# The FFN of a decoder block by 2x2 blocks with seven block products, its inner layer kept in DRAM

## The chip, the core and the metric

The kernel runs on one core of a Trainium2 chip. The metric is the device time of one execution in microseconds. The engines named below are TensorE (PE: matrix products into PSUM; PEld is its weight load), VectorE (DVE), ScalarE (ACT), GpSimd (POOL) and SyncE (SP, which here issues the DMA transfers).

## The reference

One decoder layer on x of 1024 tokens by 1024 channels, in float32: three token mixers, gated and merged, an output projection, and then the part that the change touches, a convolutional gated MLP of 2816 inner channels:

```python
    x = x + rms_norm(mixed @ w_out[l], post_mix_norm[l])
    h = rms_norm(x, pre_ffn_norm[l])
    u = causal_dwconv(h @ ffn_w_up[l], ffn_conv_w[l], ffn_conv_b[l])   # [1024, 5632], 3 taps along the tokens
    gate, val = jnp.split(u, 2, axis=-1)
    f = (jax.nn.gelu(gate, approximate=True) * val) @ ffn_w_down[l]    # [1024, 2816] @ [2816, 1024]
    x = x + rms_norm(f, post_ffn_norm[l])
```

## The kernel before

Everything is kept transposed: channels on the 128 partitions, the 1024 tokens along the free dimension, in two halves of 512. [...] `load_w` loads one unit of weights by an SP DMA, takes hi on ACT (L269) and lo on POOL (L270), or on DVE where it is given its tiles. `fm_unit` runs the matmuls of one unit of 128 output channels over `nk` input tiles (L205 is the helper that records each).

`tail_stage` holds the merge of the branches, the output projection with its norms (by halves of the sequence; the rows of x1 go to DRAM as `x1_d`), and the FFN. The FFN's input is `h2[h, k]`, a (hi, lo) pair for each half h and input tile k of 8. The inner layer has 22 tiles of 128 channels. For tile f, `up` takes two units, gate and value: 8 k x 3 matmuls x 2 halves each, 96 in all; then the convolution of three taps (`conv`: ACT L303 for the first tap, DVE L307 and L309 for the two others, `halo` being the columns that the second half needs of the first), the gelu on ACT (L1338), the product on DVE (L1345), and the split into `mhi` and `mlo` (L1346, L1347), which stay in SBUF. `down(ci, ms)` follows each chunk of `DOWN`: eight units of output channels, `nf` x 3 matmuls x 2 halves each, added to `acc` in SBUF by DVE (L1358; the first chunk is copied by ACT, L1356). The products of chunk 16 to 17 are run last but one, after the last tile's `up`; the last chunk is run by pieces of the sequence (`LAST`: 512, 256, 256 tokens), each followed by the last norm, the residual from `x1_d` and the output.

The first four tiles (`N_FIRST`) are run by halves, because the second half of the sequence is still being normalised. Within each engine the order is set by a scheduler that goes by the order of the program text, dependencies and a timeline of its own; pools of tiles (`bufs`) decide how far an engine can run ahead. All the FFN's loads go through the one queue of SP, in order.

Of the kernel before, what the change touches and what calls it, by code (L numbers as in the profile page):

```python
# [27 lines left out]
# columns of the per-channel parameter table  # L28
# [12 lines left out]
def consts():  # L41
# [18 lines left out]
    # rows 64..127 of the keys' operand: position, ones, blocks, ones for the two maxima  # L60
# [7 lines left out]
    # the queries' side of position and ones, [q, tile, head, 3], each exact in bfloat16  # L68
# [5 lines left out]
    # bias of the compressed scores, [g, tile, q, head, 64]; slot 0 is empty  # L74
# [5 lines left out]
    # blocks that are always or never taken: factor and addend, [tile, q, 2, 16]  # L80
# [12 lines left out]
def layout(a):  # L93
    """The arrays as the program takes them: transposed, cut and repeated only."""
    def units(w, cols, width=128):
        # [k*128+p, cols] -> [unit, p, k*width+c]
        w = w[:, cols]
        k = w.shape[0] // 128
        u = w.shape[1] // width
        return np.ascontiguousarray(  # L100
            w.reshape(k, 128, u, width).transpose(2, 1, 0, 3).reshape(u, 128, k * width))

    def per_channel(v):
        # [..., n*128] -> [128, n * ...]
        v = v.reshape(-1, v.shape[-1] // 128, 128) if v.ndim > 1 else v.reshape(1, -1, 128)
        return v.transpose(2, 1, 0).reshape(128, -1)
# [21 lines left out]
    # parameters by channel, in the order of the units  # L128
# [13 lines left out]
    # down: [chunk, unit, p, k*128+c], chunks of DCH tiles of the hidden layer  # L142
# [16 lines left out]
DOWN = [(0, 4), (4, 4), (8, 4), (12, 4), (16, 2), (18, 4)]  # L159
# [3 lines left out]
# The merge gates' projection units: up to which one they go with the sparse attention, the heads of the  # L163
# stick-breaking attention and the groups of the state space mixer.
# [3 lines left out]
# steps of projections traced with each step of the mixers, and the order of the latter's units  # L168
# [22 lines left out]
# the output: after which tile of a piece the one before is finished, and the tiles of one transfer  # L191
T_AT = 3
T_DMA = ((0, 4), (4, 8)), ((0, 2), (2, 4), (4, 6), (6, 8))
# [3 lines left out]
def trunk(ctx: ExitStack, tc: tile.TileContext, A: dict, outT: bass.AP, dbg=None):  # L197
# [36 lines left out]
    def rsqrt_mean(r, v, ps, n):  # L234
        """r = (ps / n + eps) ** -0.5, by exp and log and one step of Newton's; v is scratch."""
# [37 lines left out]
    def fm_unit(pool, w, rhs, nk, halves=(0, 1)):  # L273
        """ps[feature, t] of one unit of 128 features, by halves of the sequence; rhs(k, half) -> (hi, lo)."""
# [11 lines left out]
    def half_unit(pool, w, rhs, nk, h, out):  # L286
        """The same of one half, in steps of one k."""
# [12 lines left out]
    def conv(o, h, ps, taps, bias, halo):  # L300
        """o[:, t] = bias + sum of taps[d] * ps[:, t - d], for half h of the sequence; o is its part of the output"""
# [46 lines left out]
    def tm_part(ci, p, eng):  # L348
        """A quarter of the rows of a chunk of the token-major weights"""
# [37 lines left out]
    def first_half(h, tiles):  # L387
        """Input scaled by channel, split, and its squares' sum"""
# [22 lines left out]
    def norm(h, ss):  # L411
        """By token: the scale of the queries, and of the input on every partition"""
# [35 lines left out]
    def unit_steps(u, evict):  # L448
        """A projection unit by halves; a step is one half with what takes it from PSUM."""
# [6 lines left out]
    def fine_steps(u, evict):  # L456
        """The same, a step being one k of a half."""
# [6 lines left out]
    class Fill:  # L464
        """Projection steps, traced between those of the mixers."""
# [28 lines left out]
    eac = keep.tile([128, 8, 16], F32, name="eac")       # exp of the log-decay from the chunk's start  # L494
    eend = keep.tile([128, 8, 16], F32, name="eend")     # the same of the whole chunk, on every partition
# [49 lines left out]
def nsa_stage(nc, tc, es, env, start):  # L545
# [4 lines left out]
    V_hi = kp.tile([128, 8, 2, 2, 65], R32, name="V_hi")  # [key, tile, sel/win, group, value | 1]  # L550
# [51 lines left out]
    for s in range(2):  # L602
        # two positions at a time: [parity of the position | channel] on the partitions
# [15 lines left out]
        # one row for each block of each group, and one between the groups that nothing uses  # L619
# [27 lines left out]
    # the keys of one group at a time; the second's wait in DRAM  # L647
# [63 lines left out]
    def compressed(g, i):  # L711
# [61 lines left out]
        # the queries' operands of the two other branches  # L773
# [16 lines left out]
    def maxima(g, i):  # L790
        """The rows' maxima, into the operands."""
# [39 lines left out]
    def attend():  # L831
        """Scores by key, weights, values: one block of keys a step, None where there is none."""
# [80 lines left out]
    for n in range(-2, 17):  # L913
# [38 lines left out]
def sb_stage(nc, tc, es, env):  # L952
# [42 lines left out]
    def chain(h, c, ps_z, ps_out, q_hi, q_lo, k_hi, k_lo, v_hi, v_lo):  # L995
        """One head's queries of half c, from the last block of keys to the first."""
# [11 lines left out]
        def strict(x, kb):  # L1008
            # x >= 0, perhaps infinite; zero where the key isn't before the query
# [5 lines left out]
        def score(kb):  # L1015
# [6 lines left out]
            # softplus  # L1022
# [10 lines left out]
        def carry(kb):  # L1033
# [10 lines left out]
            # the softplus of this key and all between it and the query, to be taken from the scores  # L1044
# [50 lines left out]
def ssd_stage(nc, tc, es, env):  # L1095
# [8 lines left out]
    def scan(q, fill, x0, x1, B, C, z0, z1):  # L1104
# [6 lines left out]
        def front(c):  # L1111
# [8 lines left out]
            # token-major x and B, C.B by group  # L1120
# [54 lines left out]
        # gate, norm over the group's 256 channels  # L1175
# [24 lines left out]
def tail_stage(nc, tc, es, env):  # L1200
# [10 lines left out]
    def lo_t(dt=R32):  # L1211
        return mp.tile([128, 512], dt, name="lo", bufs=17)
# [11 lines left out]
    def load_y(k):  # L1224
        # the first ones take the place of what the mixers have done with
# [39 lines left out]
    up_ = es.enter_context(tc.tile_pool(name="up", side="right", reuse_waits="tile", bufs=U_BUFS))  # L1265
    op = ExitStack()
    ow = op.enter_context(tc.tile_pool(name="ow", reuse_waits="tile", bufs=2))
    for h in range(2):
        o = ow.tile([128, 8, 512], F32, name="o")

        def sumsq(sums, src, eng=V):
            """sums[0] += src^2; None for the first"""
# [16 lines left out]
        for j in range(8):  # L1289
            ps, = fm_unit(psd, load_w(A["wo"][j], 1024), lambda k, _: mix[h, k], 8, halves=(h,))  # L1290
            act(o[:, j, :], ps, AF.Copy)
# [3 lines left out]
        for j in range(8):  # L1295
            x = ow.tile([128, 512], F32, name="ox", bufs=8)
            nc.sync.dma_start(x, A["xT"][j * 128:(j + 1) * 128, hs(h)])
            V.scalar_tensor_tensor(o[:, j, :], o[:, j, :], pvc(PV_PM, j), r, op0=OP.mult, op1=OP.mult)
# [23 lines left out]
    def h2_rhs(k, h):  # L1322
        return h2[h, k]

    def up(f, st, halves=(0, 1)):
# [13 lines left out]
        if halves[-1] == 0:  # L1339
            return  # L1340
# [9 lines left out]
    def down(ci, ms, also=None):  # L1350
        nf = DOWN[ci][1]
        for j in range(8):
# [6 lines left out]
            if also:  # L1359
                also(j)  # L1360
# [97 lines left out]
```

## Time and profile before

| | |
|---|---|
| time, median of 3 | 2348.51 us (2346.61 to 2348.75) |
| the profiled execution | span 2347.0 us from the first to the last instruction; no other time was taken of it |
| PE busy | 2261.6 us, 96% |
| DVE, ACT, POOL busy | 1311.3, 1055.4, 912.3 us |
| mean granted TensorE clock | 0.988 |
| DMA, mean over the span | 74 GB/s |
| out-projection and norms | about 1461 to 1640 us |
| FFN | from about 1580 us; its last chunk from about 2275 us |

The profile is of one execution. A row of its groups gives the line, the engine, the operation, output and input tiles, shapes and count, then busy time and the mean of one in ns, then the engine's idle time just before these and what ended it. A window's row gives busy time and number of instructions for each engine. Matmuls are pipelined: a record is longer than the time between two of them. Engines work at the same time, so that busy shares do not add up.

### The profile page before, as it was taken

What the parts mean: (1) busy time and instruction counts of PE and PEld (TensorE: products, weight loads), DVE (VectorE), ACT (ScalarE), POOL (GpSimd) and SP (SyncE); (2) the same over time, 40 slices, a digit from 0 to 9 for tenths busy, and PEclk for the clock granted to TensorE, in tenths of its full rate; (3) what the DMA queues carried; (4) which work ended last, traced back from release to release, by engine and by line L of the source; (5) the groups of instructions that cost most, each with busy time, mean ns of one, the idle gap of its engine ahead of it and who ended that gap; (6) DMA issues with size and microseconds to landing.
All of it is one profiled execution on the core that took longest, in us unless ns stands there. A gap on an engine that the chain in (4) does not pass through costs nothing.

```text
span 2347.0 us, 29315 instructions
## 1 busy us (share of the span) xinstructions
PE 2261.6 (96%) x11020; PEld 1828.0 (78%) x11020; DVE 1311.3 (56%) x2351; ACT 1055.4 (45%) x1842; POOL 912.3 (39%) x671
## 2 busy tenths in 40 slices
PE   8999999999999999999998999998999999999997
PEld 7997666667887788778786888876788888888886
DVE  8324875781476676565757443378714343443556
ACT  7144665666466766444443322345433131322334
POOL 4122565565233324553535264455422221222213
PEclk9999999999999999999999999998999999999998
DMA  5233112101111112021212462343221111112132
GB/s 191 81 88 96 48 40 69 57 8 59 37 54 46 46 45 72 32 77 41 77 53 83 159 202 97 117 152 111 78 63 41 59 41 50 54 32 67 46 117 72
DMA packets 90126, 173.49 MB, mean 74 GB/s; under 512 B 25280, under 2 KB 39296, under 8 KB 89984
## 3 DMA queue, kind: packets, MB, share of 16 engines
q1 hardware_dynamic: 89696, 171.39, 22.4%
q8 instruction: 87, 1.43, 0.2%
q14 instruction: 55, 0.45, 0.1%
q10 hardware_dynamic: 288, 0.22, 0.0%
HBM read 138.55 MB, written 33.03 MB: 73 GB/s over the span
## 4 chain that ended last, share of the span: by engine, by line
PE 82%; DVE 11%; ACT 3%; issue 2%; POOL 2%; DMA 1%; SPq 0%; DVEq 0%; ACTq 0%; POOLq 0%
PE dense L205 66%; PE ps_s L205 5%; PE ps_o L205 4%; PE ps_t L205 4%; PE ps_b L205 2%; DVE mx L813 2%; POOL wlo L270 1%; DVE row L307 1%; DVE o L1306 1%; ACT whi L269 0%; DVE acc L1410 0%; POOL R L1116 0%; DVE xe L1138 0%; POOL osq L1278 0%; DVE cp L733 0%
## 5 line engine op out<-in xcount | busy, mean ns | idle before, releaser
L270 POOL TENSOR_TENSOR wlo<-wraw,whi 128x1024 fp32r<-128x1024 f32 (+2 forms) x194 | 405.5, 2092 | 837.1 <-ACT whi L269 799.7
L205 PE MATMUL dense<-h_hi,whi 128*128 128x512 f32 x992 | 401.6, 405 | 3.5 <-DVE row L307 3.4
L205 PE MATMUL dense<-h_lo,whi 128*128 128x512 f32 x992 | 393.4, 397 | 0.0
L205 PE MATMUL dense<-h_hi,wlo 128*128 128x512 f32 x992 | 392.0, 395 | 0.0
L269 ACT ACTIVATE whi<-wraw 128x1024 fp32r<-128x1024 f32 (+2 forms) x194 | 179.2, 925 | 386.0 <-PE dense L205 350.2
L205 PE MATMUL dense<-hi,whi 128*128 128x512 f32 x832 | 326.6, 393 | 11.2 <-ACT whi L269 11.2
L205 PE MATMUL dense<-hi,wlo 128*128 128x512 f32 x832 | 327.0, 394 | 4.4 <-POOL wlo L270 4.3
L205 PE MATMUL dense<-lo,whi 128*128 128x512 f32 x832 | 326.0, 392 | 1.5 <-POOL lo L1313 1.5
L205 PEld LDWEIGHTS dense<-h_hi,whi 128*128 128x128 f32 x992 | 188.3, 190 | 44.4 <-ACT sa L1026 3.6
L205 PEld LDWEIGHTS dense<-h_hi,wlo 128*128 128x128 f32 x992 | 187.6, 189 | 40.0 <-issue 1.1
L205 PEld LDWEIGHTS dense<-h_lo,whi 128*128 128x128 f32 x992 | 188.3, 190 | 36.0 <-issue 1.8
L307 DVE SCALAR_TENSOR_TENSOR u<-dense,pv,u 128x511 f32<-128x511 f32 (+1 forms) x176 | 130.8, 743 | 133.3 <-ACT u L303 132.0
L853 POOL TENSOR_TENSOR wT_lo<-wT,wT_hi 128x512 fp32r<-128x512 f32 x132 | 169.2, 1292 | 86.7 <-ACT wT_hi L852 80.2
L205 PEld LDWEIGHTS dense<-hi,whi 128*128 128x128 f32 x832 | 157.5, 189 | 46.2 <-ACT whi L269 13.4
L205 PEld LDWEIGHTS dense<-hi,wlo 128*128 128x128 f32 x832 | 157.4, 189 | 40.6 <-POOL wlo L270 7.2
L205 PEld LDWEIGHTS dense<-lo,whi 128*128 128x128 f32 x832 | 157.4, 189 | 35.3 <-POOL lo L1313 2.4
L205 PE MATMUL dense<-mhi,whi 128*128 128x512 f32 x288 | 112.2, 392 | 0.3
L205 PE MATMUL dense<-mlo,whi 128*128 128x512 f32 x288 | 112.3, 390 | 0.0
L1043 POOL TENSOR_TENSOR s_lo<-sa,s_hi 128x512 fp32r<-128x512 f32 (+2 forms) x48 | 53.8, 1125 | 148.9 <-ACT s_hi L1042 137.6
L842 ACT ACTIVATE wT<-ps_s 128x512 f32<-128x512 f32 x132 | 78.4, 594 | 68.3 <-PE ps_s L205 63.6
L205 PE MATMUL dense<-mhi,wlo 128*128 128x512 f32 x288 | 105.6, 389 | 0.0
L813 DVE TENSOR_REDUCE mx<-ps_t 128x1 f32<-128x384 f32 (+3 forms) x192 | 93.9, 514 | 18.1 <-PE ps_t L205 15.9
(377 smaller groups left out, 4560.8 us busy)
## 6 DMA issues: line engine op xcount, KB each, us to landing
wraw<-in_wfm SPq DMA_DIRECT2D x62, 512.0 KB, 3.4
wraw<-in_wup SPq DMA_DIRECT2D x52, 512.0 KB, 3.3
g_d<-gate_e SPq DMA_DIRECT2D x48, 256.0 KB, 2.1
ge<-g_d SPq DMA_DIRECT2D x24, 512.0 KB, 3.9
wraw<-in_wo SPq DMA_DIRECT2D x16, 512.0 KB, 3.4
wraw<-in_wdn SPq DMA_DIRECT2D x32, 256.0 KB, 2.6
yraw<-y_d SPq DMA_DIRECT2D x12, 512.0 KB, 4.2
x<-in_xT SPq DMA_DIRECT2D x16, 256.0 KB, 5.5
```

The lines of the kernel that those rows point to most:

```text
L205: i = f(*a, **k)
L269: act(hi, raw, AF.Copy)
L270: (V if tiles else P).tensor_tensor(lo, raw, fl(hi), op=OP.subtract)
L307: V.scalar_tensor_tensor(o[:, d:], ps[:, :512 - d], taps[d], o[:, d:], op0=OP.mult, op1=OP.add)
L813: V.tensor_reduce(mx[:, h, a, n:n + 1], pm[:, :w], axis=AX, op=OP.max)
L842: act(w.rearrange("p h q -> p (h q)"), pz, AF.Exp)
L853: P.tensor_tensor(lo, wf, fl(hi), op=OP.subtract)
L1043: (P if SB_SLO else V).tensor_tensor(s_lo[:, c0:], a[:, c0:], fl(s_hi[:, c0:]), op=OP.subtract)
L1306: i = V.scalar_tensor_tensor(o[:, j, :], o[:, j, :], pvc(PV_FFN, j), r, op0=OP.mult, op1=OP.mult)
```

## The change

A product of matrices cut into 2x2 blocks needs eight block products; after combining blocks by additions beforehand and adding up the results, seven do. The change uses this twice, with fifteen additions of blocks in its form.

In the up projection the 2x2 blocks of the weights are (gate, value) by (input tiles 0 to 3, 4 to 7), and those of the input are (input tiles 0 to 3, 4 to 7) by (first, second half of the sequence). `up_pair` runs 7 products x 4 tiles x 3 = 84 matmuls for a tile of the inner layer. It does so for 18 of the 22 tiles; the first four are run by halves as before. The combinations of the input are made once (`combos`, on DVE). Those of the weights are made for each tile by `weights7`, the four additions and the lo parts on POOL, the hi parts on ACT. The results are put together in three PSUM banks x, y, z: the bank x goes on collecting products, and ACT copies its state (`snap`) at three points.

All tiles' `up` now comes first. The inner layer goes to DRAM (`m_d`) in float32, half a tile at a time, and is read back chunk by chunk. `DOWN` is cut into chunks of 2, 4, 4, 4, 4 and 4 tiles. For the first five, `m_rhs` combines (POOL) and splits (ACT hi, DVE lo) the inner layer's blocks, and `down_pair` computes two units of output channels at once by seven products: 42 matmuls instead of 48 in a chunk of four, 21 instead of 24 in that of two. The results are added to `acc` by DVE (from PSUM) and by POOL (the copies). The last chunk is run by pieces as before, with its inner layer and weights loaded, and split by ACT and DVE, behind the fifth chunk. x1 is read by two transfers of 2 MB in place of 16 of 256 KB, placed in the SP queue ahead of the last four units' weights; the output leaves by one transfer per unit and piece. The ring of lo tiles has 16 buffers instead of 17, that of the convolution's tiles 4 instead of 6.

The diff, cut to its core (its other lines only remove comments or rename the pieces of the last chunk):

```diff
-DOWN = [(0, 4), (4, 4), (8, 4), (12, 4), (16, 2), (18, 4)]
+DOWN = [(0, 2), (2, 4), (6, 4), (10, 4), (14, 4), (18, 4)]
-U_BUFS = 6
+U_BUFS = 4
...
+    def weights7(src0, src1, n):
+        raws = []
+        for m, src in enumerate((src0, src1)):
+            raw = (wx if turn[0] % 3 == 2 else E.wp).tile([128, 1024], F32, name="wraw", bufs=1 + (turn[0] % 3 < 2))[:, :2 * n]
+            turn[0] += 1
+            nc.sync.dma_start(raw, src)
+            raws.append(raw)
+        a11, a12, a21, a22 = [r[:, s] for r in raws for s in (slice(0, n), slice(n, 2 * n))]
+        whi, wlo = [E.wp.tile([128, 1024], R32, name=f"w{x}", bufs=2)[:, :2 * n] for x in ("hi", "lo")]
+        ahi, alo = [wx.tile([128, 512], R32, name=f"a{x}", bufs=1)[:, :n] for x in ("hi", "lo")]
+        act(whi, raws[0], AF.Copy)
+        P.tensor_tensor(wlo, raws[0], fl(whi), op=OP.subtract)
+        f31, f24 = [wx.tile([128, 1024], F32, name=f"uf{x}", bufs=1)[:, :2 * n] for x in range(2)]
+        (h31, l31), (h24, l24) = [[wx.tile([128, 1024], R32, name=f"u{x}")[:, :2 * n] for x in ("hi", "lo")]
+                                  for _ in range(2)]
+        u3, u1, u2, u4 = [x[:, s] for x in (f31, f24) for s in (slice(0, n), slice(n, 2 * n))]
+        P.tensor_tensor(u1, a21, a22, op=OP.add)
+        P.tensor_tensor(u2, u1, a11, op=OP.add)
+        P.tensor_tensor(u4, u2, a12, op=OP.add)
+        act(h24, f24, AF.Copy)
+        P.tensor_tensor(l24, f24, fl(h24), op=OP.subtract)
+        P.tensor_tensor(u3, a11, a21, op=OP.add)
+        act(h31, f31, AF.Copy)
+        P.tensor_tensor(l31, f31, fl(h31), op=OP.subtract)
+        act(ahi, a22, AF.Copy)
+        P.tensor_tensor(alo, a22, fl(ahi), op=OP.subtract)
+        lo, up = slice(0, n), slice(n, 2 * n)
+        return {1: (whi[:, lo], wlo[:, lo]), 2: (whi[:, up], wlo[:, up]), 3: (h24[:, up], l24[:, up]),
+                4: (ahi, alo), 5: (h31[:, up], l31[:, up]), 6: (h24[:, lo], l24[:, lo]), 7: (h31[:, lo], l31[:, lo])}
+
+    def product(ps, w, rhs, q, first):
+        hi, lo = w[q]
+        for k, b in enumerate(rhs[q]):
+            s = slice(k * 128, (k + 1) * 128)
+            for n, (x, y) in enumerate(((hi, b[0]), (hi, b[1]), (lo, b[0]))):
+                mm(ps, x[:, s], y, start=first and k == 0 and n == 0, stop=k == len(rhs[q]) - 1 and n == 2,
+                   skip_group_check=True)
+
+    def snap(ps):
+        s = up_.tile([128, 512], F32, name="snap", bufs=5)
+        act(s, ps, AF.Copy)
+        return s
...
+    def up_pair(f, rhs):
+        st = {}
+        w = weights7(A["wup"][2 * f], A["wup"][2 * f + 1], 512)
+        x, y, z = bank(), bank(), bank()
+        product(x, w, rhs, 1, True)
+        s1 = snap(x)
+        product(y, w, rhs, 2, True)
+        V.tensor_tensor(y, y, s1, op=OP.add)
+        conv(2 * f, 0, y, st)
+        product(x, w, rhs, 6, False)
+        s2 = snap(x)
+        product(z, w, rhs, 7, True)
+        s7 = snap(z)
+        product(x, w, rhs, 5, False)
+        s3 = snap(x)
+        P.tensor_tensor(s7, s7, s3, op=OP.subtract)
+        product(z, w, rhs, 4, False)
+        V.tensor_tensor(z, z, s2, op=OP.subtract)
+        conv(2 * f + 1, 0, z, st)
+        gated(f, 0, st)
+        product(x, w, rhs, 3, False)
+        conv(2 * f + 1, 1, s7, st)
+        conv(2 * f, 1, x, st)
+        gated(f, 1, st)
...
+    for f in range(N_FIRST, NFF):
+        up_pair(f, rhs)
...
+    def m_rhs(f0, nf):
+        rhs = {q: [] for q in range(1, 8)}
+        n = nf // 2
+        for k in range(n):
+            b11, b12 = [m_tile(f0 + k, h, 0) for h in range(2)]
+            b21, b22 = [m_tile(f0 + n + k, h, 1) for h in range(2)]
+            t3, t2, t1, t4 = [up_.tile([128, 512], F32, name="snap", bufs=5) for _ in range(4)]
+            for q in range(1, 8):
+                rhs[q].append((x_t() if q == 1 else hi_t(), x_t() if q == 1 else lo_t()))
+            P.tensor_tensor(t3, b12, b22, op=OP.subtract)
+            P.tensor_tensor(t2, t3, b11, op=OP.subtract)
+            P.tensor_tensor(t1, b11, b12, op=OP.subtract)
+            P.tensor_tensor(t4, t2, b21, op=OP.add)
+            for q, src in ((1, b11), (2, b21), (6, t2), (7, t3), (5, t1), (4, t4), (3, b22)):
+                hi, lo = rhs[q][k]
+                act(hi, src, AF.Copy)
+                V.tensor_tensor(lo, src, fl(hi), op=OP.subtract)
+        return rhs
+
+    def down_pair(ci, j, rhs):
+        n = DOWN[ci][1] // 2 * 128
+        w = weights7(A[f"wdn{ci}"][j], A[f"wdn{ci}"][j + 1], n)
+        c11, c12, c21, c22 = [acc[h][j + m] for m in range(2) for h in range(2)]
+        x, y, z = bank(), bank(), bank()
+        product(x, w, rhs, 1, True)
+        s1 = snap(x)
+        product(y, w, rhs, 2, True)
...
+            V.tensor_tensor(c11, c11, y, op=OP.add)
+            P.tensor_tensor(c11, c11, s1, op=OP.add)
+        product(x, w, rhs, 6, False)
+        s2 = snap(x)
+        product(z, w, rhs, 7, True)
...
+            V.tensor_tensor(c22, c22, z, op=OP.add)
+        product(x, w, rhs, 5, False)
+        s3 = snap(x)
+        P.tensor_tensor(c22, c22, s3, op=OP.subtract)
+        product(z, w, rhs, 4, False)
...
+            V.tensor_tensor(c21, c21, z, op=OP.add)
+            P.tensor_tensor(c21, c21, s2, op=OP.subtract)
+        product(x, w, rhs, 3, False)
...
+            V.tensor_tensor(c12, c12, x, op=OP.add)
...
+    x1s = [x1p.tile([128, 8, 512], F32, name=f"x1_{h}") for h in range(2)]
+    for h in range(2):
+        nc.sync.dma_start(x1s[h], E.x1_d[:, hs(h)].rearrange("(a p) t -> p a t", p=128))
```

More of the change, by code (lines that the diff above doesn't have):

```diff
@@ L192 @@
 T_AT = 3
-T_DMA = ((0, 4), (4, 8)), ((0, 2), (2, 4), (4, 6), (6, 8))
 @with_exitstack
@@ new lines, in combos, with conv @@
+    def combos(b11, b12, b21, b22, eng):
+        eng.tensor_tensor(b22, b12, b22, op=OP.subtract)
+        eng.tensor_tensor(b12, b11, b12, op=OP.subtract)
+        eng.tensor_tensor(b11, b22, b11, op=OP.subtract)
+        eng.tensor_tensor(b21, b11, b21, op=OP.add)
+    m_d = E.scratch("m_d", [NFF * 128, T])
+    def conv(u, h, ps, st):
+        s = u % 2
+        if h == 0:
+            st["halo", s] = up_.tile([128, 4], F32, name="halo", bufs=12)
+        st[s, h] = up_.tile([128, 512], F32, name=f"u{s}")
+        E.conv(st[s, h], h, ps, [pvc(PV_FW, 3 * u + 2 - d) for d in range(3)], pvc(PV_FB, u), st["halo", s])
+        if s == 0:
+            act(st[0, h], st[0, h], AF.Gelu_apprx_tanh)
@@ new lines, in tail_stage, with m_tile @@
+    for q, k, t, place in sorted(later, key=lambda x: (-x[0], x[1])):
+        rhs[q][k] = hi, lo = place(), x_t()
+        act(hi, t, AF.Copy)
+        V.tensor_tensor(lo, t, fl(hi), op=OP.subtract)
+    for f in range(N_FIRST, NFF):
+        up_pair(f, rhs)
+    acc = []
+    def m_tile(f, h, s):
+        t = up_.tile([128, 512], F32, name=f"u{s}")
+        nc.sync.dma_start(t, m_d[f * 128:(f + 1) * 128, hs(h)])
+        return t
+    def m_rhs(f0, nf):
[16 more added lines that the diff above has]
+        return rhs
@@ new lines, in w_split @@
+    def w_split(j, place):
+        ws.append(load_w(A[f"wdn{last}"][j], 512, place, up_.tile([128, 512], F32, name="snap", bufs=5)))
+    for k in range(nf):
+        m_split(k, 0)
+    for j in range(4):
+        w_split(j, (x_t(), x_t()))
+    for k in range(nf):
+        m_split(k, 1)
+    for j in range(4, 8):
+        w_split(j, (hi_t(), lo_t()))
+    wx_.close()
+    x1p = es.enter_context(tc.tile_pool(name="x1", reuse_waits="tile", bufs=1))
+    x1s = [x1p.tile([128, 8, 512], F32, name=f"x1_{h}") for h in range(2)]
@@ L1390, in tail_stage @@
+    for h in range(2):
+        nc.sync.dma_start(x1s[h], E.x1_d[:, hs(h)].rearrange("(a p) t -> p a t", p=128))
     ended = None
@@ L1422, in tail_stage @@
         for j in range(8):
-            ps = psd.tile([128, 512], F32, name="dense", tag="dense")
+            ps = bank()
             hi, lo = ws[j]
```

174 lines of the change are left out of this document (88 added, 86 removed).

## The prediction

> **What bounds the kernel now.** I read the head of the page first, then its chain of waits, then PE's waits, the table by stage and the groups of the FFN.
>
> ```profile
> span 2347.0 us, 29315 instructions
> PE 2261.6 (96%) x11020; PEld 1828.0 (78%) x11020; DVE 1311.3 (56%) x2351; ACT 1055.4 (45%) x1842; POOL 912.3 (39%) x671
> PE 82%; DVE 11%; ACT 3%; issue 2%; POOL 2%; DMA 1%; SPq 0%; DVEq 0%; ACTq 0%; POOLq 0%
> PE dense L205 <- ACT whi L269: 8.7, 4, 3.7
> PE dense L205 <- POOL wlo L270: 4.3, 4, 1.9
> 1575.00:1650.00 75.00, 62.43 (x241) 47.78 (x241) 68.22 (x76) 38.63 (x55) 43.01 (x21) 0.91 0.29 98
> 1850.00:1950.00 100.00, 100.00 (x443) 82.86 (x442) 41.85 (x69) 29.04 (x39) 23.07 (x11) 1.00 0.16 53
> 1950.00:2275.00 325.00, 324.82 (x1432) 268.51 (x1431) 145.38 (x240) 94.75 (x134) 72.23 (x41) 1.00 0.19 59
> ```
>
> PE is busy in 96% of the span and is 82% of the chain that ended last. The waits are PE's from 1575 us to 2300 us, where the FFN is: 8.7 us for `whi` and 4.3 us for `wlo`, all near its start. The columns of the last three rows are the stretch, its length, then busy time and instructions of PE, PEld, DVE, ACT and POOL, then the granted clock. From 1650 us on PE is full at a clock of 1.00. POOL is busy 23.07 of 100 us, 22% in the long stretch; DVE about 45%. So PE bounds the FFN alone, POOL and DVE have room, and a matmul less is worth its issue time until another engine fills. That issue time:
>
> ```profile
> 1663.74 0.39 PE L205 MATMUL dense<-hi,wlo 128*128 128x512 f32 x1
> 1665.78 0.39 PE L205 MATMUL dense<-hi,wlo 128*128 128x512 f32 x1
> ```
>
> Nine matmuls start in 2.04 us: 0.2267 us each (the 0.39 us overlap). The span is 1.5 us under the median of the three times (2348.51); I sum on the span and add 1.5 at the end. A difference of 0.2%, 4.7 us, is about what a measurement of this kernel can tell from none.
>
> **Up projection: what it saves.** Four tiles keep their 96 matmuls. Eighteen go from 96 to 7 products x 4 k x 3 = 84: 216 fewer, 216 x 0.2267 = **-49.0 us**, if PE stays the bound at 84 x 0.2267 = 19.04 us a tile. The others' work needs prices:
>
> ```profile
> L270 POOL TENSOR_TENSOR wlo<-wraw,whi 128x1024 fp32r<-128x1024 f32 x53 | 129.3, 2440 | 310.3 <-ACT whi L269 310.3
> L270 POOL TENSOR_TENSOR wlo<-wraw,whi 128x512 fp32r<-128x512 f32 x32 | 41.2, 1293 | 160.8 <-ACT whi L269 160.8
> L270 POOL TENSOR_TENSOR wlo<-wraw,whi 128x256 fp32r<-128x256 f32 x8 | 6.4, 802 | 31.8 <-ACT whi L269 26.5 <-PE dense L205 5.3
> L1413 POOL TENSOR_TENSOR acc<-hi,acc 128x512 f32<-128x512 f32 x8 | 10.6, 1364 | 36.7 <-DVE acc L1410 36.7
> L1413 POOL TENSOR_TENSOR acc<-lo,acc 128x256 f32<-128x256 f32 x11 | 7.6, 724 | 5.4 <-DVE acc L1410 5.4
> L1345 DVE TENSOR_TENSOR u<-u,u 128x512 f32<-128x512 f32 x44 | 30.9, 703 | 1.4
> L1347 DVE TENSOR_TENSOR mlo<-u,mhi 128x512 fp32r<-128x512 f32 x44 | 30.1, 690 | 24.5 <-ACT mhi L1346 24.5
> L307 DVE SCALAR_TENSOR_TENSOR u<-dense,pv,u 128x511 f32<-128x511 f32 x88 | 65.5, 744 | 132.0 <-ACT u L303 132.0
> L1358 DVE TENSOR_TENSOR acc<-acc,dense 128x512 f32<-128x512 f32 x64 | 43.4, 686 | 93.8 <-PE dense L205 93.7
> L269 ACT ACTIVATE whi<-wraw 128x1024 fp32r<-128x1024 f32 x52 | 55.0, 1057 | 88.4 <-PE dense L205 86.0 <-issue 2.3
> L269 ACT ACTIVATE whi<-wraw 128x512 fp32r<-128x512 f32 x32 | 19.9, 630 | 96.5 <-PE dense L205 96.5
> L1356 ACT ACTIVATE acc<-dense 128x512 f32<-128x512 f32 x16 | 9.4, 589 | 18.6 <-PE dense L205 18.6
> ```
>
> Per tile `weights7` and the subtraction in `up_pair` give POOL three instructions of 1024 columns and six of 512: 3 x 2.4 + 6 x 1.29 = 14.9 us, where before it had two `wlo`, 4.9 us. Some eight DVE instructions per tile read two SBUF operands (two products, two of the convolution on a copied bank, four halo columns). Those and POOL hold each other up:
>
> ```profile
> 1602.32 11.09 DVE L1298 SCALAR_TENSOR_TENSOR o<-o,pv,orstd 128x512 f32<-128x512 f32 x7
> 1602.49 1.73 POOL L1300 TENSOR_TENSOR o<-o,ox 128x512 f32<-128x512 f32 x1 [3.20 <-DVE o L1298]
> 1604.19 2.84 POOL L270 TENSOR_TENSOR wlo<-wraw,whi 128x1024 fp32r<-128x1024 f32 x1
> 1606.99 1.75 POOL L1300 TENSOR_TENSOR o<-o,ox 128x512 f32<-128x512 f32 x1
> 1608.69 2.85 POOL L270 TENSOR_TENSOR wlo<-wraw,whi 128x1024 fp32r<-128x1024 f32 x1
> L1313 POOL TENSOR_TENSOR lo<-o,hi 128x512 fp32r<-128x512 f32 x8 | 13.7, 1730 | 3.4 <-ACT hi L1309 3.4
> L1315 DVE TENSOR_TENSOR lo<-o,hi 128x512 fp32r<-128x512 f32 x8 | 9.0, 1129 | 0.0
> ```
>
> Seven DVE instructions that take about 0.7 us alone take 11.09 us, because each waits for the POOL instruction in progress, and POOL's take 1.73 to 1.75 instead of 1.29 and 2.84 instead of 2.4. So a meeting costs POOL 0.44 us and DVE up to POOL's rest. L1313 and L1315 show the same at 1730 and 1129 ns. Four long meetings and four short ones make some 2.2 us: POOL 17.1 of 19.04 us. The order of POOL's stream lets the split of a tile's last factor begin only when the tile before has ended its product 3, but it is needed 8.2 us later and takes 2.4, so PE does not wait. DVE needs about 10 us (two sums on a bank at 0.69, eight convolution steps at 0.74, two products at 0.70, halos) and, at up to 1.2 us for a meeting, some 6.6 of waits; ACT about 10.5 (two `whi`-sized rows, `ahi`, three copies, four convolutions, two gelus). The cover for the saving is thus 2 us of POOL per tile. For the first pair, whose nine POOL instructions start behind the last ordinary `wlo`, I add 2 us (0 to 6).
>
> **First tiles to pairs.** Behind the first four tiles' second half DVE gets 16 combinations and 16 low parts with two SBUF operands: 32 x 0.69 = 22 us alone, 32 x 1.13 = 36 us by L1315, ahead of or between the convolutions that free PE's banks, in a stretch of 192 x 0.2267 = 43.5 us on PE. In the row 1575 to 1650 above DVE is already busy 68.22 of 75 us. The convolutions there need some 24 us more, so the overrun is between 0 and about 20 us; much of the low parts is wanted only by products 5 and 4. I take **+8 us**, nearer to the cheap end, because the order has the last eight low parts behind the convolutions.
>
> **Down projection: what it costs.** PE needs 756 matmuls in place of 864 for these 18 tiles (24.5 us less): 42 x 0.2267 = 9.5 us for a pair of output tiles in a chunk of four. POOL's share of such a pair, at the rows above: `wlo` 1.29, four additions of 256 columns 2.96, two low parts of 512 2.58, `alo` 0.74, and the three additions to `acc` that the change gives POOL, 3.87: 11.4 us. Each chunk adds 8 combinations in `m_rhs`, 10.3 us. So POOL needs 4 x 11.4 + 10.3 = 56 us a chunk, PE 38.1 and before 43.5: **POOL is the bound of the down projection.** The chunk of two tiles is 4 x 5.8 + 5.2 = 28 us (128 columns estimated at 0.45 us, by continuing 1.29 and 0.74), and four chunks of four 224: 252 us. About 5 us of the first weights lie ahead, inside the up projection: 247. Neighbouring POOL rows above overlap by 0.03 us (1602.49 + 1.73 against 1604.19), so it may be 7 less; I take off half: 243.
>
> On top come the meetings. `m_rhs` has DVE split 14 low parts a chunk, 7 in the small one: 63 instructions of two SBUF operands into a POOL that never rests, 63 x 0.44 = 28 us (bounds 0 and 44: none met, or POOL stopped for the whole 0.69). DVE's additions of a bank to `acc` read PSUM, like L1358, which stays at 686 beside `wlo`; I charge them nothing. Waits of POOL for PE's copies within a pair: the subtraction of s3 comes 3.3 us behind the last low part, which PE follows with two products, 2.7 us, and a copy, 0.59: 0.3 us each, some 4 us in all. The first combinations wait about 1 us for the last hidden tile from DRAM, and PE ends its last products 5 us behind POOL. Sum 243 + 28 + 4 + 1 + 5 = 281 us, against 864 x 0.2267 = 196 before: **+85 us**. ACT (about 25 us a chunk) and DVE (about 30) stay behind POOL.
>
> [...]
>
> **Last chunk.** Its matmuls stay. The weights of output tiles 4 to 7 queue on SP behind two loads of x1 of 2 MB each:
>
> ```profile
> wraw<-in_wup SPq DMA_DIRECT2D x52, 512.0 KB, 3.3
> wraw<-in_wdn SPq DMA_DIRECT2D x32, 256.0 KB, 2.6
> ```
>
> The second 256 KB of a load cost 0.7 us, so 4 MB are about 16 x 0.7 + 1.9 = 13 us; with load and split the fifth tile's weights are there 15 us after PE starts the piece and wanted after 4 x 12 x 0.2267 = 10.9: 4 us. Against that, some start ahead. I take 3 (0 to 6), and 0.5 for eight small output transfers per piece: **+3.5 us**. The stores to `m_d` and loads from it wait on SP ahead of weight loads, whose buffers run one tile ahead; at 2.6 us a load against 19 us a tile I charge nothing, and a late one would cost 2 to 3 us.
>
> Sum: 2347.0 - 49.0 + 2 + 8 + 85 + 3.5 = 2396.5 us of span; with 1.5, **2398 us**.
>
> **The rivals.** *Full lock.* As the forecast, but every meeting costs POOL 0.69 us: 16 us more, 2414. For it: POOL never rests in the down projection. Against it: the rows 1602.49 to 1608.69. [...]
>
> [...] If DVE's two-operand instructions (some 3.7 us a tile) exclude POOL's 14.9 entirely and each hand-over costs a little, the tile takes 21 us in place of 19.04: 18 x 2 = 36 us, and 2434. It decides where POOL and DVE's share pass 19 us; 18.6 is close.
>
> *Cheap meetings.* DVE's low parts fall where POOL waits anyway, and the transition is free: 2398 - 28 - 4 - 8 - 2 - 3.5 = 2352 (2346 to 2358 by the overlap of POOL's rows). Against it: POOL has no idle time for them to fall into.
>
> *Faster: PE stays the bound of the down projection.* Place: POOL's stream per pair. If POOL's 128x512 additions ran as fast as DVE's 0.69, a chunk would be 30 us on POOL, PE's 38.1 would bound, and 324 matmuls would be saved: 2347 - 73.5 + 13.5 + 1.5 = 2288. The gain decides from 245 us: below 196 + 49 for the whole down projection it is faster. Against it: L270 and L1413, a subtraction and an addition, at 1293 and 1364.
>
> **How the numbers follow.** Forecast 0.52 (its own range 2375 to 2412), full lock 0.12, port in the up projection 0.16, cheap meetings 0.11, faster 0.05; 0.04 for something slower still. The range must leave out 0.2: it leaves out the gain, a part of the cheap case and the slowest: 2349 to 2440. The cheap case is split over both sides of the 0.2% bound. Faster 0.06, same 0.04, slower 0.90.
>
> **What would show it.** Right: POOL at 95% or more from the end of the up projection to the last chunk, at about 281 us for it; PE there at about 60%, waiting for POOL's `ulo` and `wlo`; L1486's DVE low parts at 1.1 us or more; PE full in the up projection with 19.0 us a tile. Wrong: PE busy over 90% in the down projection; a tile of the up projection at 21 us; POOL rows of 128x512 well under 1.29 us.

## The result, and the profile after

The changed kernel takes 2412.3 us (median of 4, 2411.9 to 2412.7) beside 2347.9 for the kernel before: 1.0274 times as long, 95% interval 1.0259 to 1.0288. The forecast was 2398, in a range of 2349 to 2440. The profiled execution spans 2410.8 us, 63.8 more than before.

The head of the page and the chain of waits of the changed kernel, then PE's granted clock in 40 slices:

```profile
span 2410.8 us, 29759 instructions
PE 2239.7 (93%) x10696; PEld 1778.6 (74%) x10696; DVE 1488.8 (62%) x2454; ACT 1186.2 (49%) x2085; POOL 1335.7 (55%) x1005
PE 69%; DVE 13%; POOL 7%; issue 5%; ACT 4%; DMA 2%; SPq 0%; DVEq 0%; POOLq 0%; ACTq 0%
PEclk9999999999999999999999999989999999888888
```

PE has 21.9 us less to do and its share of the chain falls from 82% to 69%; POOL's rises from 2% to 7%, and POOL is busy 423 us more. The clock, at 1.00 in the kernel before from 1650 to 2275 us, is below 0.9 in the last six slices, from about 2050 us on. The table by stage (columns as before: stretch, length, busy time and instructions of PE, PEld, DVE, ACT, POOL, granted clock):

```profile
1740.00:2040.00 300.00, 300.00 (x1325) 248.43 (x1324) 210.48 (x286) 155.63 (x223) 249.68 (x143) 1.00 0.24 80
2040.00:2088.00 48.00, 35.61 (x133) 23.91 (x131) 25.67 (x41) 28.11 (x56) 35.44 (x46) 0.96 0.36 118
2152.00:2215.00 63.00, 47.91 (x168) 34.09 (x168) 31.05 (x30) 22.73 (x42) 56.42 (x53) 0.84 0.21 67
2215.00:2278.00 63.00, 46.58 (x168) 33.20 (x168) 31.89 (x30) 23.13 (x43) 56.96 (x53) 0.86 0.21 67
```

In the first row, the up projection by pairs, PE is full and POOL busy in 83%: 19.0 us a tile, as forecast. The second holds the start of the down projection: PE is busy 35.6 of 48 us. The third and fourth are one chunk of four tiles each: 168 matmuls in 63 us, where the kernel before had 192 in 43.5. Four rows of PE's waits over the FFN, with what ended them (total, times, longest), the two largest first:

```profile
PE dense L204 <- DVE lo L1486: 24.2, 9, 4.5
PE dense L204 <- ACT hi L1485: 19.5, 7, 5.5
PE dense L204 <- POOL wlo L269: 9.0, 4, 5.0
PE dense L204 <- POOL ulo L1353: 3.3, 7, 1.0
```

Both kernels hold each factor in two parts, hi and lo, lo being the value less hi, and a product of two tiles is three matmuls (hi·hi, hi·lo, lo·hi). Counting the matmul records of both traces gives the parts. From the first pair on (1694.1 us before, 1700.8 after) the transition has cost 6.7 us; the eighteen tiles take 351 us for 391.7, that is 40.7 less; the down projection of the first eighteen tiles takes 289.6 us for 197.6, 92.0 more; the last chunk and the end take 69.2 for 63.6, 5.6 more. Together 63.6 us. In the down projection (2051.8 to 2341.6 us) POOL is busy 257.5 us, 89%, and PE 217.6, 75%.

### The profile page after: what moved, and what is told of

Same layout as the page of the kernel before. It is cut to its first block, busy times and chain, and to the rows that moved or that the text cites. A ratio compares the mean times of both kernels' runs of the same rounds, so it can differ in the third digit from the quotient of the medians.

```text
span 2410.8 us, 29759 instructions
## 1 busy us (share of the span) xinstructions
PE 2239.7 (93%) x10696; PEld 1778.6 (74%) x10696; DVE 1488.8 (62%) x2454; ACT 1186.2 (49%) x2085; POOL 1335.7 (55%) x1005
## 4 chain that ended last, share of the span: by engine, by line
PE 69%; DVE 13%; POOL 7%; issue 5%; ACT 4%; DMA 2%; SPq 0%; DVEq 0%; POOLq 0%; ACTq 0%
PE dense L204 53%; PE ps_s L204 5%; PE ps_o L204 4%; PE ps_t L204 4%; PE ps_b L204 2%; DVE mx L812 2%; DVE lo L1486 1%; POOL wlo L269 1%; POOL wlo L1344 1%; DVE x L1313 1%; POOL ulo L1353 1%; DVE row L306 1%; DMA wraw<-in_wdn 1%; POOL alo L1358 1%; DMA snap<-in_wdn 1%
## 5 line engine op out<-in xcount | busy, mean ns | idle before, releaser
L269 POOL TENSOR_TENSOR wlo<-wraw,whi 128x1024 fp32r<-128x1024 f32 (+1 forms) x118 | 279.8, 2372 | 378.6 <-ACT whi L268 369.2
L204 PEld LDWEIGHTS dense<-h_hi,whi 128*128 128x128 f32 x992 | 187.6, 189 | 44.4 <-ACT sa L1025 3.5
L268 ACT ACTIVATE whi<-wraw 128x1024 fp32r<-128x1024 f32 (+1 forms) x118 | 117.8, 999 | 205.9 <-PE dense L204 191.4
L204 PE MATMUL dense<-lo,whi 128*128 128x512 f32 x436 | 176.1, 404 | 15.8 <-DVE lo L1486 13.7
L204 PE MATMUL dense<-hi,wlo 128*128 128x512 f32 x436 | 177.0, 407 | 9.8 <-POOL wlo L269 9.0
L204 PE MATMUL dense<-hi,whi 128*128 128x512 f32 x436 | 174.9, 403 | 10.3 <-ACT whi L268 10.3
L204 PE MATMUL dense<-hi,uhi 128*128 128x512 f32 x288 | 121.6, 425 | 37.0 <-ACT hi L1485 19.5
L204 PE MATMUL dense<-hi,ulo 128*128 128x512 f32 x288 | 117.7, 411 | 5.7 <-POOL ulo L1353 3.3
L204 PE MATMUL dense<-x,uhi 128*128 128x512 f32 x360 | 117.0, 390 | 1.5 <-ACT uhi L1352 1.3
L204 PEld LDWEIGHTS dense<-hi,whi 128*128 128x128 f32 x436 | 85.0, 195 | 31.3 <-ACT whi L268 12.8
L306 DVE SCALAR_TENSOR_TENSOR u<-dense,pv,u 128x510 f32<-128x510 f32 (+1 forms) x140 | 101.8, 736 | 6.4 <-ACT u L302 6.3
```

The costliest lines, as they stand in the source:

```text
L204: i = f(*a, **k)
L268: act(hi, raw, AF.Copy)
L269: (V if tiles else P).tensor_tensor(lo, raw, fl(hi), op=OP.subtract)
L306: V.scalar_tensor_tensor(o[:, d:], ps[:, :512 - d], taps[d], o[:, d:], op0=OP.mult, op1=OP.add)
```

## The experiments

Each was run beside the kernel before on the same chip. What is given as over or under before is the difference of the two medians of that run.

**The parts alone.** In `up7_down8` the five chunks are computed by eight products from the inner layer read back:

```diff
-        rhs = m_rhs(f0, nf)
+        parts = [[(hi_t(), lo_t()) for _ in range(2)] for _ in range(nf)]
+        for h in range(2):
+            for k in range(nf):
+                src, (hi, lo) = m_tile(f0 + k, h, k % 2), parts[k][h]
+                act(hi, src, AF.Copy)
+                V.tensor_tensor(lo, src, fl(hi), op=OP.subtract)
...
-        for j in range(0, 8, 2):
-            down_pair(ci, j, rhs)
+        for j in range(8):
+            pss = fm_unit(psd, load_w(A[f"wdn{ci}"][j], nf * 128), lambda k, h: parts[k][h], nf)
+            for h, ps in enumerate(pss):
...
+                    V.tensor_tensor(acc[h][j], acc[h][j], ps, op=OP.add)
```

> Seven products in the up projection alone; the down projection of the first five chunks by eight products, its inner layer still read back from DRAM (split by ACT and DVE, 8 parts of half a tile per chunk). Theory A (the loss lies in the down projection, where POOL is the bound; the up projection gains what its matmuls say): up projection as in the changed kernel, down projection back to 864 x 0.2267 = 196 us with some 5 us for the start of the first chunk, last chunk as changed: 2412 - (290 - 201) = about 2323 us, 25 us faster than before. Rival B (the way through DRAM and the order, all up tiles first, is what costs): less than 30 us come back, 2380 or more.

Measured: 2330.5 us, 18.1 under before (ratio 0.9924, 0.9909 to 0.9939). So the up projection's seven products do make the kernel faster, and the down projection's take that back. It missed the 2323 by 7 us: one gap of 10.3 us at the start of the down projection.

In `up8_down7` it is the other way round, and the combinations of the up projection's input go:

```diff
-    rhs = {q: [None] * 4 for q in range(1, 8)}
...
     for f in range(N_FIRST, NFF):
-        up_pair(f, rhs)
+        st = {}
+        for s in range(2):
+            w = load_w(A["wup"][2 * f + s], 1024)
+            for h in range(2):
+                ps, = fm_unit(psd, w, lambda k, h: h2[h, k], 8, halves=(h,))
+                conv(2 * f + s, h, ps, st)
+        for h in range(2):
+            gated(f, h, st)
```

> Seven products in the down projection alone; the up projection by eight, all tiles first, inner layer through DRAM. Theory A: the up projection loses its 41 us of gain and the 7 us of the transition go too: 2412 + 41 - 7 = about 2446 us. Rival (up and down share a burden, so that parts do not add): under 2425.

Measured: 2442.6 us, 94.0 over before (1.0399, 1.0384 to 1.0415). The parts add to within 4 us: 94.0 - 33.8 (the up projection's gain, below) is 60, and both together measured 64.

**What holds the down projection.** `acc_dve` moves POOL's three additions a pair:

```diff
-            P.tensor_tensor(c11, c11, s1, op=OP.add)
+            V.tensor_tensor(c11, c11, s1, op=OP.add)
...
-        P.tensor_tensor(c22, c22, s3, op=OP.subtract)
+        V.tensor_tensor(c22, c22, s3, op=OP.subtract)
...
-            P.tensor_tensor(c21, c21, s2, op=OP.subtract)
+            V.tensor_tensor(c21, c21, s2, op=OP.subtract)
```

> The changed kernel with the three additions of copied banks to acc in each pair on DVE instead of POOL. Theory A (POOL's stream sets the 11.0 us of a pair): POOL has 7.6 us a pair and some 1.3 of meetings, under PE's 9.5; a pair takes 9.5 to 10 us, the chunk 63.3 - 6 or more; with the first chunk about 2412 - 28 = 2384 us (2370 to 2390). Rival C (the pair is set by a chain from POOL's low part through PE's products, ACT's copy and the addition, wherever the addition runs): within 8 us of 2412.

Measured: 2389.0 us, 40.5 over before (1.0172, 1.0155 to 1.0189): 24 us less than the changed kernel, of 28 expected. So a chain that is as long wherever the additions run (rival C) is out, and work taken from POOL shortens the kernel. `lo_psum` leaves POOL's work alone and removes its meetings with DVE's low parts of the inner layer. It subtracts a bank of zeros in place of `hi`: the kernel leaves out the true low parts, so that its output is not the layer's, and these instructions no longer wait for ACT's `hi` either.

```diff
+    zero = psn.tile([128, 512], F32, name="psn", tag="psn")
+    act(zero, h2[0, 0][0].bitcast(F32), AF.Copy, scale=0.0)
...
-                V.tensor_tensor(lo, src, fl(hi), op=OP.subtract)
+                V.tensor_tensor(lo, src, zero, op=OP.subtract)
```

> The changed kernel with the low parts of the inner layer in the five chunks taken as src minus a bank of zeros in PSUM, so that DVE reads one operand from SBUF and never meets POOL there; the low parts are then not the low parts, the instructions are as many and as long. Theory D (at the start of each chunk DVE's low parts are held up by POOL's stream, 7.38 us for one, and PE waits for them and then runs at half clock): the 19.3 us between the last pair of a chunk and the second of the next fall to 12 to 14, 4 x 6 + 4 = 25 to 30 us: about 2385. Rival (the start of a chunk is set by POOL's combinations and by the tiles that the last pair holds): less than 8 us.

Measured: 2388.6 us, 40.0 over before (1.0171, 1.0155 to 1.0186). The stretch of one chunk in its trace, and DVE's low parts there:

```profile
2141.40:2196.00 54.60, 43.31 (x170) 31.47 (x169) 19.37 (x30) 22.70 (x42) 53.89 (x53) 0.97 0.24 77
2196.00:2250.50 54.50, 43.09 (x169) 31.45 (x168) 19.32 (x30) 22.70 (x42) 53.84 (x53) 0.97 0.24 78
L1488 DVE TENSOR_TENSOR lo<-snap,psn 128x512 fp32r<-128x512 f32 x36 | 23.6, 684 | 28.6 <-POOL snap L1482 18.2 <-POOL snap L1484 10.3
```

POOL is busy 53.9 of 54.6 us with its 53 instructions: without meetings it is the bound of these chunks. That is 8.5 us a chunk less than in the changed kernel, where POOL is busy 56.4 to 57.0 of 63 us with as many, and where the same 36 low parts have this row:

```profile
L1486 DVE TENSOR_TENSOR lo<-snap,hi 128x512 fp32r<-128x512 f32 x36 | 59.9, 1705 | 17.3 <-ACT hi L1485 17.3
```

1705 ns for 684. How much of the 8.5 us is the wait for `hi` is not told apart. `acc_psum` then takes the additions from POOL and from SBUF at once: DVE adds bank x to acc while PE goes on in another bank, and ACT's copies go.

```diff
         product(x, w, rhs, 1, True)
-        s1 = snap(x)
+        if ci == 0:
+            s1 = snap(x)
+        else:
+            V.tensor_tensor(c11, c11, x, op=OP.add)
...
-            P.tensor_tensor(c11, c11, s1, op=OP.add)
...
-        s2 = snap(x)
+        if ci == 0:
+            s2 = snap(x)
+        else:
+            V.tensor_tensor(c21, c21, x, op=OP.subtract)
...
-        s3 = snap(x)
-        P.tensor_tensor(c22, c22, s3, op=OP.subtract)
+        V.tensor_tensor(c22, c22, x, op=OP.subtract)
...
-            P.tensor_tensor(c21, c21, s2, op=OP.subtract)
```

> The changed kernel with the partial sums of the second to fifth chunk added to acc by DVE straight from bank x in PSUM, in place of ACT's copies and POOL's (in acc_dve: DVE's) additions of them. POOL's stream is then 7.3 us a pair and 39.5 a chunk, and the additions meet nothing, unlike those of acc_dve. Theory A: a pair falls under PE's 9.5 us and PE or the start of the chunk binds; a chunk takes 38 to 40 us of matmuls and 8 to 12 of its start, 48 to 52 in place of 63.3: about 2412 - 52 = 2360 us, well under acc_dve's 2389. Rival C (the pair is bound otherwise): within 8 us of acc_dve. By either it stays behind up7_late's 2322, whose chunk takes 43.5.

Measured: 2365.8 us, 15.9 over before (1.0070, 1.0054 to 1.0086), 48 us under the changed kernel by the differences to before. Fifty us of its trace, across the first and the second full chunk, and PE's two largest waits:

```profile
2150.00:2200.00 50.00, 42.71 (x165) 32.71 (x164) 33.49 (x42) 16.60 (x29) 44.41 (x40) 0.92 0.25 76
PE dense L204 <- ACT uhi L1352: 9.2, 4, 4.0
PE dense L204 <- DVE x L1508: 8.5, 4, 4.0
```

POOL is busy in 44.4 of 50 us, DVE 33.5, PE 42.7, and PE now waits for several of them a little. The four full chunks take 66.6, 50.3, 50.8 and 42.2 us; eight products take 43.5. Only the fourth, which has no next chunk's combinations beside it, comes under that.

**The way through DRAM, and a version that is faster.** In `up7_down8` PE stood still at 2051 us. SP's queue had the two loads of x1, 2 MB each, among those of the inner layer's first tiles (issued at 2050.6 and 2052.6 us), and four of the last chunk's weights ahead of them. `up7_late` queues x1, in pieces of 256 KB, and the last chunk's inner layer and weights behind the fourth chunk's last weights (`load_w.ins` is the load that `load_w` issued last):

```diff
+            if ci == last - 2:
+                mark = load_w.ins
...
+    with tc.issue_after(mark):
...
-            nc.sync.dma_start(x1s[h], E.x1_d[:, hs(h)].rearrange("(a p) t -> p a t", p=128))
+            for j in range(8):
+                nc.sync.dma_start(x1s[h][:, j], E.x1_d[j * 128:(j + 1) * 128, hs(h)])
```

> Seven products in the up projection, eight in the down projection as in up7_down8, and the loads of x1 (by 256 KB again) and of the last chunk's weights queued on SP behind the last weights of the fourth chunk. In up7_down8 PE waits 10.7 us at the start of the down projection for the first tiles of the inner layer, which stand on SP behind the first 2 MB of x1. Theory: that gap falls to 2 to 5 us, two smaller ones of 2.75 and 1.65 us go with it: 2330.5 - 8 = about 2322 us. Rival (the tiles themselves are late, since the last pair holds their buffers): 2327 or more.

Measured: 2321.7 us, 28.4 under before: 0.9879, 0.9864 to 0.9894. It beats both kernels. PE's waits at that place, first in `up7_down8`, then in `up7_late`, and the stages of the latter:

```profile
PE dense L204 <- ACT hi L1531: 10.3, 1, 10.3
```

```profile
PE dense L204 <- ACT hi L1531: 1.9, 2, 1.4
1740.00:2040.00 300.00, 300.00 (x1325) 248.40 (x1324) 210.38 (x286) 154.95 (x223) 250.30 (x145) 1.00 0.24 80
2056.00:2275.00 219.00, 216.68 (x945) 177.99 (x946) 88.15 (x132) 67.89 (x117) 47.10 (x38) 0.99 0.38 120
```

The gap of 10.3 us is now two of 1.9 in all, and PE is busy 99% or more of both stretches at a clock of 0.99 to 1.00. Which of the loads that were moved had held it is not told apart. `up8_late` is the same with the up projection of `up8_down7`.

> The same with eight products everywhere: only the order (all up tiles first), the inner layer's way through DRAM and the last chunk's changes are left of the change. Theory: the way through DRAM costs next to nothing while PE is full, 2348 + 2 to 7: about 2353 us; then up7_late minus this one is the up projection's gain, 49 - 15 of stalls at its start = some 33 us. Rival (the way through DRAM costs 10 us or more): above 2358.

Measured: 2355.5 us, 5.4 over before (1.0027, 1.0017 to 1.0037). The order, the way through DRAM and the last chunk's changes cost that much together, and the seven products of the up projection gain 28.4 + 5.4 = 33.8 us.

**The transition and the last chunk.** `up7_late_comb` moves the input's combinations:

```diff
-        combos(*lows, V)
+        combos(*lows, P)
```

> up7_late with the 16 combinations of the up projection's input on POOL instead of DVE. In the changed kernel's trace POOL's wlo at 1659.8 us takes some 7.6 us beside DVE's run of combinations, and PE waits 5.0 us for it. Theory E (a run of DVE instructions with two SBUF operands keeps POOL out): that wait goes, 2 to 6 us less than up7_late. Rival (POOL's own 16 x 1.29 = 21 us then delay its wlo and the first pairs' weights): 0 to 10 us more.

Measured: 2328.5 us, 21.6 under before (0.9909, 0.9894 to 0.9923), 7 more than `up7_late`: the rival. PE's waits for `wlo` grow from 5.0 us to 8.0:

```profile
PE dense L204 <- POOL wlo L269: 8.0, 4, 4.7
```

`up7_late_wlo` moves the other side, the `wlo` of the first tiles' second half, to DVE:

```diff
-        (V if tiles else P).tensor_tensor(lo, raw, fl(hi), op=OP.subtract)
+        (V if tiles or on_v else P).tensor_tensor(lo, raw, fl(hi), op=OP.subtract)
...
-            ps, = fm_unit(psd, load_w(A["wup"][u], 1024), lambda k, h: h2[h, k], 8, halves=(h,))
+            ps, = fm_unit(psd, load_w(A["wup"][u], 1024, on_v=h == 1), lambda k, h: h2[h, k], 8, halves=(h,))
```

> up7_late with the low parts of the first four tiles' weights on DVE for the second half of the sequence, behind its combinations in order, so that POOL has nothing there that DVE's run can keep out. Theory E (POOL kept out by that run): PE's wait of 5.0 us for wlo goes; DVE gets 8 x 1.4 = 11 us more, of which some shows: 2318 to 2322 us against 2321.7. Rival (DVE is full there): 2326 or more.

Measured: 2322.1 us, 27.8 under before (0.9887, 0.9868 to 0.9905), no change that can be told. The wait of 5.0 us goes, and others come:

```profile
PE dense L204 <- ACT snap L1376: 9.0, 3, 8.6
PE dense L204 <- DVE wlo L269: 3.9, 4, 1.3
```

That POOL was kept out is seen in the rows of the next section; this run shows that taking the wait away gains nothing. The work costs as much with these low parts on DVE, and 7 us more with the combinations on POOL. `x1_behind` is the changed kernel with

```diff
-    for h in range(2):
-        nc.sync.dma_start(x1s[h], E.x1_d[:, hs(h)].rearrange("(a p) t -> p a t", p=128))
+    with tc.issue_after(load_w.ins):
+        for h in range(2):
+            nc.sync.dma_start(x1s[h], E.x1_d[:, hs(h)].rearrange("(a p) t -> p a t", p=128))
```

> The changed kernel with the two loads of x1 of 2 MB queued on SP behind the last chunk's last four weights instead of ahead. Theory: PE's 2.9 us of waiting for ACT's hi (L268) in the last chunk, and what it takes from the clock, go: about 2409 us. Rival (the weights' buffers are the limit, not the queue): no change.

Measured: 2407.2 us, 57.1 over before (1.0243, 1.0226 to 1.0260), some 5 to 7 us less than the changed kernel. PE's wait for ACT's `hi` (L268), 2.9 us in the changed kernel's last chunk, is gone. From the last chunk's first matmul to the end its trace has 64.1 us for 69.2, so the difference lies there; the kernel before has 63.6.

## Why the prediction was right, point by point

*The up projection: right.* 216 matmuls are gone, POOL stays under PE, and a tile takes 19.0 us. The rival of 21 us a tile, which was an estimate, is out: POOL is busy 249.7 of 300 us, 15.8 a tile where I had 17.1, and PE 300.0. Mis-sized was the start of the pairs: 2 us in the sum, some 8 in the trace, of which four waits of PE of 0.8 to 2.0 us in the first two pairs make 5.6.

*First tiles to pairs: the size right (8, measured 6.7), the place not, so that the size is luck.* I had PE wait for banks that a late DVE frees. It waited 5.0 us for POOL's `wlo` instead, which DVE's run of combinations kept out:

```profile
1659.82 7.24 POOL L269 TENSOR_TENSOR wlo<-wraw,whi 128x1024 fp32r<-128x1024 f32 x1 [7.15 <-ACT whi L268]
...
1661.14 0.68 DVE L1452 TENSOR_TENSOR x<-x 128x512 fp32r<-128x512 f32 x1
1661.75 0.68 DVE L1382 TENSOR_TENSOR x<-x 128x512 f32<-128x512 f32 x1
1662.35 0.68 DVE L1452 TENSOR_TENSOR x<-x 128x512 fp32r<-128x512 f32 x1
1662.95 0.67 DVE L1382 TENSOR_TENSOR x<-x 128x512 f32<-128x512 f32 x1
...
1667.11 0.80 PE L204 MATMUL dense<-hi,wlo 128*128 128x512 f32 x1 [4.97 <-POOL wlo L269]
```

A `wlo` of 2.4 us takes 7.24 us, while eight of DVE's two-operand instructions start every 0.60 us and do not wait.

*The down projection: right in the main, 92 us for 85.* POOL binds it in the middle of a chunk, where its instructions follow each other without a gap, and a pair takes 11.0 us, for 11.4 at full durations:

```profile
2127.59 1.27 POOL L1501 TENSOR_TENSOR x<-x,snap 128x512 f32<-128x512 f32 x1
2128.82 0.73 POOL L1358 TENSOR_TENSOR alo<-wraw,ahi 128x256 fp32r<-128x256 f32 x1
2129.53 1.29 POOL L1517 TENSOR_TENSOR x<-x,snap 128x512 f32<-128x512 f32 x1
2130.78 1.28 POOL L1353 TENSOR_TENSOR ulo<-uf,uhi 128x512 fp32r<-128x512 f32 x1
...
2138.60 1.28 POOL L1501 TENSOR_TENSOR x<-x,snap 128x512 f32<-128x512 f32 x1
```

From L1501 at 2127.59 to the next at 2138.60, each instruction but one begins 0.02 to 0.04 us before the one ahead of it ends. Four full chunks take 253 us; the sum has about 254 for them. What was too small is the first chunk with its start: about 27 us in the sum, 36.4 in the trace. I had 1 us for the last inner tile from DRAM; PE stood still for 4.3 us there and then in eight gaps of 0.4 to 1.5 us: a pair of this chunk has half the matmuls, but as many instructions for its weights. Two of the signs that I named did not come. I expected POOL at 95% or more and PE at 60%, waiting for POOL's `ulo` and `wlo`; POOL has 89% and PE 75%, and PE waits most for DVE's low parts and ACT's `hi`, 24.2 and 19.5 us, for `ulo` 3.3.

*The meetings: the size right, the way half right.* The sum has 28 us; in `lo_psum` the four full chunks are 31 us shorter, of which it gave 5 back in its last chunk. In the changed kernel's four full chunks 42 of POOL's 203 instructions are lengthened, by 0.43 us on average, as I had priced a meeting: 18 us. But POOL also stands idle for 25 us there, and 18 of them, at the start of the second to fourth of these chunks, are not in the sum. In `lo_psum` the two are 2.9 and 8.7 us. At such a start POOL has a row of instructions ready, and DVE does not get in:

```profile
2154.63 7.38 DVE L1486 TENSOR_TENSOR lo<-snap,hi 128x512 fp32r<-128x512 f32 x1 [4.24 <-ACT hi L1485]
2155.12 1.27 POOL L1353 TENSOR_TENSOR ulo<-uf,uhi 128x512 fp32r<-128x512 f32 x1
2156.36 1.27 POOL L1356 TENSOR_TENSOR ulo<-uf,uhi 128x512 fp32r<-128x512 f32 x1
2157.59 1.28 POOL L1482 TENSOR_TENSOR snap<-snap,u 128x512 f32<-128x512 f32 x1
2158.83 1.28 POOL L1479 TENSOR_TENSOR snap<-u,u 128x512 f32<-128x512 f32 x1
2160.06 0.72 POOL L1349 TENSOR_TENSOR uf<-wraw 128x256 f32<-128x256 f32 x1
2160.74 0.72 POOL L1354 TENSOR_TENSOR uf<-wraw 128x256 f32<-128x256 f32 x1
2162.76 1.59 POOL L1480 TENSOR_TENSOR snap<-snap,u 128x512 f32<-128x512 f32 x1 [1.29 <-DVE lo L1486]
2164.31 1.71 POOL L1481 TENSOR_TENSOR snap<-u,u 128x512 f32<-128x512 f32 x1
2155.17 0.79 PE L204 MATMUL dense<-hi,uhi 128*128 128x512 f32 x1 [5.51 <-ACT hi L1485]
2162.67 0.80 PE L204 MATMUL dense<-lo,uhi 128*128 128x512 f32 x1 [3.18 <-DVE lo L1486]
```

A low part is begun at 2154.63 and ends 7.38 us later (the two behind it take 0.68 each), when POOL's stream comes to an instruction that waits for it. POOL loses nothing up to there: 1.27 us a piece. PE does: in its second row it waits 3.18 us for these low parts, and another gap of 3.61 follows. POOL's later instructions then wait for ACT, which waits for PE. From 2162.76 on the two engines take turns, and POOL's pieces take 1.59 and 1.71 us in place of 1.28: that is the meeting of the forecast, and of its rows from 1602 us on, where four of the seven DVE instructions wait (1.78 to 2.88 us each) and three do not (0.74 and 0.75). So my price for the meetings was about right, but some half of the time comes as idle time of POOL, by a way that the sum does not have; that the chunks lose about its 28 us all the same is luck. The full lock (0.69 us a meeting, 44 us, 2414 in all) gave the time to 2 us, but not for its reason: none of POOL's 42 is lengthened by more than 0.48 us, and the 14 us by which the forecast fell short lie elsewhere. The measured time is at the upper end of the forecast's own range, 2375 to 2412.

*The last chunk: 3.5 forecast, 5.6 measured.* The place was right: with x1 queued behind the weights (`x1_behind`) 5.1 of the 5.6 us are gone.

*The other rivals.* Meetings are not cheap: `lo_psum`, without them and without the wait for `hi`, takes 24 us less than the changed kernel. That PE stays the bound of the down projection needs POOL below PE: even in `acc_psum`, which leaves POOL 39.5 us a chunk by the sum, it was busy longer than PE, 44.4 of 50 us for 42.7. The break-even of that rival, 245 us for the whole down projection, leaves out the sum's other 13.5 us: it is 231.5. Measured were 289.6, so that nothing hangs on it.

## What to carry to other kernels

Count what a saving on the full engine asks of the others in the stage where it asks it, not over the kernel: POOL was busy 15.8 us a tile against 19.0 of PE in the up projection by seven products, and 56.4 to 57.0 of the 63 us of a chunk, for which PE's matmuls ask 38.1, in the down projection, where a pair has half the matmuls and the inner layer's combinations and the sums to acc come on top. Look for places where DVE and POOL both read two operands from SBUF: here a run of ready instructions on one kept the other waiting for the whole run, 7.38 us for an instruction of 0.68 and 7.24 for one of 2.4; in `lo_psum`, with an operand in PSUM, the low parts took 684 ns in place of 1705. And queue what is wanted late behind what is wanted soon: that was worth 10 us between `up7_down8` and `up7_late`.

## What the runs showed of the hardware

In the changed kernel a DVE instruction that reads two SBUF operands waited through six POOL instructions (7.38 us for 0.68, from 2154.63 us), and a POOL instruction through eight of DVE's (7.24 us for 2.4, from 1659.82 us). In `lo_psum`, with one operand in PSUM, the 36 low parts took 684 ns on average beside POOL's stream, for 1705 in the changed kernel. Where the two took turns, DVE waited for the end of POOL's instruction: one begun at 2163.14 us took 1.76 us for 0.68 and ended 0.55 us behind the POOL instruction of 2162.76. The meeting cost POOL 0.43 us on average (42 instructions of the four full chunks, 0.48 at most), not DVE's whole 0.68. Who was next differed: in the two places of 7.38 and 7.24 us it was the engine with the run of ready instructions, to the run's end; from 2162.76 us on in the changed kernel, and from 1602.49 in the kernel before, the two took turns. When which of these occurs, the runs do not show.

In the changed kernel the granted clock was 0.50 from 2152.2 to 2159.0 us, around the end of PE's gap of 5.51 us at 2155.17, and, with PE's gaps of 3.18 and 3.61 us, from 2162.4 to 2176.0; between and behind these it was 1.00. At 0.50 the matmuls started half as often:

```profile
2172.42 0.63 PE L204 MATMUL dense<-hi,ulo 128*128 128x512 f32 x1
2173.70 0.63 PE L204 MATMUL dense<-hi,ulo 128*128 128x512 f32 x1
...
2178.33 0.39 PE L204 MATMUL dense<-hi,uhi 128*128 128x512 f32 x1
2179.69 0.39 PE L204 MATMUL dense<-hi,uhi 128*128 128x512 f32 x1
```

Three matmuls in 1.28 us, 0.427 each, and a few us later, at 1.00, six in 1.36, 0.227 each. No run here shows how long a gap brings the slow clock, or what that clock costs by itself.
